# Attention on one core: more exponentials on VectorE, part of its last product on GpSimd, and TensorE's work dealt out in unequal rounds

## The chip, the core and the metric

The kernel runs on one core of a Trainium2 chip. A core has five engines with queues of their own, which run side by side and wait for one another through semaphores: TensorE (PE in the profile, with its weight loads as PEld), VectorE (DVE), ScalarE (ACT), GpSimd (POOL) and SyncE (SP, which here only issues DMAs). The metric is the device time of one execution in microseconds (us); lower is better. Times are quoted as the median of a few runs, and the profile is of one execution.

## The reference, cut to what matters

Multi-query attention: 8 batches, 1024 positions, 16 query heads of 64, and one key and one value head that all query heads share.

```
scores   = q @ k.T / sqrt(64)                     # per batch and head, 1024 x 1024
weights  = exp(scores - max) / sum(exp(scores - max))
attn_out = weights @ v                            # 1024 x 64 per head
```

Everything comes in and goes out as float32. The kernel works in float16 with float32 sums, leaves the maximum out, and checks at the end that no sum has left a safe range; a general version behind a branch would compute the case where one has. The branch is not taken for this data.

## The kernel before, in words

**Steps.** Heads are taken in pairs, queries in chunks of 512, keys in blocks of 128. One *step* is one key block for one chunk of one pair: 64 pairs x 2 chunks x 8 key blocks = 1024 steps (`STEPS`). A batch is 128 steps. In a step TensorE multiplies a key block by the chunk's queries for both heads (two matmuls of 64 rows x 512 columns, L247) and so fills a score tile `sc` of 128 x 1024 float32. `sc` comes from a PSUM pool of three buffers (`scp`), so the scores of step u can only be written when the tile of step u-3 has been read.

**Two ways to the exponential.** Most steps go to ScalarE: one ACTIVATE (L260) reads `sc` and writes `wt`, 128 x 1024 float16. Every fifth step (`VE_EVERY = 5`, `to_vector`) goes to VectorE instead; I call that a *unit*, and there are 200 of them, from step 10 to step 1005. `vector_exp` computes the exponential of a unit from the bits of a float16:

1. the *eviction* (L211): `sc` to 16-bit integers in `w3[:, 1]`, which read as float16 are a piecewise linear exponential;
2. `m` (L217): its mantissa with the exponent set to zero;
3. `w0` (L227): its power of two, into `w3[:, 0]`;
4. the *square* (L235): `m2 = m * m`;
5. the *last product* (L237): `w3[:, 2] = w3[:, 1] * m2`.

The three tiles `w3[:, 0..2]` are weights of the same unit against three scaled copies of the values (`vp[:, 1]`, `vp[:, 0]`, `vp[:, 2]`), so a unit gives TensorE three matmuls where a ScalarE step gives one. The eviction is issued in its step; the other four operations wait in a list, `pend`, and `step` issues two of them per step. The last product of a unit stays in `product` until the next unit and is issued right behind that unit's eviction.

**Values.** `values` multiplies the weights of one head and 128 queries by the value rows: for each *group*, 8 matmuls plus 2 more for each unit among its chunk's 8 steps, all into one column range of a PSUM tile `ot` (L318). There are 1024 groups, as many as steps, and they run 18 steps (`LAG`) behind the scores. Seven groups share an `ot` tile; when it is full, `inverse` (L263, reciprocals of the sums) and `finish` (L272, the division, to `osb`) are put into `pend`. I call the two a *finish*; there are 146.

**The order of the work.** The order on each engine is written out by hand (`manual_schedule`): each engine runs its own instructions in the order of the program text. The main loop goes in rounds of two steps (`BATCH = 2`): both steps' scores, then any new finish, then two groups of values, then `after`, which loads and turns what the next batch needs. Near the end (`HURRY`) values run with less lag. Around the loop stand a start-up (loads, the first transposes) and an end (`last_values`, the check, the flag).

**GpSimd's queue.** It holds, in the program's order, the DMA issues of the queries (`load_q`, L121) and values (`load_v`, L104) of the next batch, and two multiplications (`prep_k`, L190) per batch that make the scaled keys. Nothing else is on it in the main loop. SyncE's queue holds the stores (L300), the key loads and the transposing DMAs.

Of the kernel before, what the change touches and what calls it, by code (L numbers as in the profile page):

```python
# [14 lines left out]
ALU = mybir.AluOpType  # L15
# [6 lines left out]
C0 = 0.9833984375  # L22
C3 = 0.163818359375
CS = 2.1471603163479376
VE_EVERY = 5


@with_exitstack
def attention_main(ctx, tc, q, k, v, out, flag):
# [38 lines left out]
    op = ctx.enter_context(tc.tile_pool(name="op", bufs=2, space=PSUM))  # L68
# [66 lines left out]
    def bank(name):  # L135
        return op.tile([P, 512], FP32, tag="ot", name=name)
# [69 lines left out]
    def vector_exp(sc, p, c, j):  # L206
        w3 = w3p.tile([P, 3, 2, QCH], FP16, tag="w3", name=f"we{p}_{c}_{j}")
        m = mp.tile([P, 2, QCH], FP16, tag="m", name=f"m{p}_{c}_{j}")
        m2 = mp.tile([P, 2, QCH], FP16, tag="m2", name=f"mm{p}_{c}_{j}")
        t = w3[:, 1].bitcast(I16)  # L210
        nc.vector.tensor_scalar(  # L211
            out=t, in0=sc, scalar1=15.0 * 1024, scalar2=0.0, op0=ALU.add, op1=ALU.max
        )
        if product:
            pend.append(product.pop())
        pend.append(
            lambda: nc.vector.tensor_scalar(  # L217
                out=m.bitcast(I16),
                in0=t,
                scalar1=0x3FF,  # L220
                scalar2=0x3C00,
                op0=ALU.bitwise_and,
                op1=ALU.bitwise_or,
            )
        )
        pend.append(
            lambda: nc.vector.tensor_scalar(  # L227
                out=w3[:, 0].bitcast(I16),
                in0=t,
                scalar1=0x7C00,  # L230
                scalar2=None,
                op0=ALU.bitwise_and,
            )
        )
        pend.append(lambda: nc.vector.tensor_tensor(out=m2, in0=m, in1=m, op=ALU.mult))  # L235
        product.append(
            lambda: nc.vector.tensor_tensor(out=w3[:, 2], in0=w3[:, 1], in1=m2, op=ALU.mult)  # L237
        )
        wt[(p, c, j)] = [(w3[:, 0], 1), (w3[:, 1], 0), (w3[:, 2], 2)]

# [21 lines left out]
    def inverse(o, g0, n):  # L262
        nc.vector.reciprocal(out=rec_all[:, g0 : g0 + n], in_=o[:, 0:n, D])  # L263

    def finish(o, g0, n):

        rec = rec_all[:, g0 : g0 + n]
        i0 = g0 % (OCH * GRP)
        if i0 == 0:
            osb[0] = osbp.tile([P, OCH * GRP, D], FP32, tag="osb", name=f"osb{g0}")  # L270
        ob = osb[0]
        nc.vector.tensor_tensor(  # L272
            out=ob[:, i0 : i0 + n, :],
            in0=o[:, 0:n, 0:D],
            in1=rec.unsqueeze(2).broadcast_to([P, n, D]),
            op=ALU.mult,
        )
        while stored[0] < g0 + n:
            e = stored[0]
            e += GRP // 2 if e >= NG - GRP else GRP  # L280
            if e > g0 + n:
                break
            store(ob, stored[0], e)
            stored[0] = e
        per = HP * NCH * GRP
        if g0 + n == NG:
            check(g0 - GRP // 2, NG, ok_all[:, B:])
        elif checked[0] < B and g0 + n >= min((checked[0] + 1) * per, NG - GRP):
            e = min((checked[0] + 1) * per, NG - GRP)
# [16 lines left out]

    def values(p, c, g):

        b = p // HP
        qb, hh = divmod(g, 2)  # L310
        gg = (p * NCH + c) * GRP + g
        if gg % GB == 0:
            ot[0] = bank(f"ot{gg}")[:, 0 : GB * 72].rearrange("p (g f) -> p g f", f=72)
        o = ot[0]
        vp = kv[b]["vp"]
        terms = [(j, w, i) for j in range(NKT) for w, i in wt[(p, c, j)]]
        for n, (j, w, i) in enumerate(terms):
            nc.tensor.matmul(  # L318
                o[:, gg % GB, 0 : D + 1],
                w[:, hh, qb * P : (qb + 1) * P],  # L320
                vp[:, i, j, 0 : D + 1],
                start=(n == 0),
                stop=(n == len(terms) - 1),
            )
        if gg % GB == GB - 1 or gg == NG - GRP - 1:
            late.append((o, gg - gg % GB, gg % GB + 1))
        if g == GRP - 1:
            for j in range(NKT):
                del wt[(p, c, j)]

    def last_values():

# [39 lines left out]
    LAG = 2 * NKT + 2  # L372
    STEPS = NP * NCH * NKT
    PSTEPS = NCH * NKT
    BATCH = 2
    LAST_VE = (STEPS - 2 * NKT) // VE_EVERY * VE_EVERY
    HURRY = STEPS - NKT - 4

    def to_vector(u):
        return u % VE_EVERY == 0 and NKT <= u <= LAST_VE  # L380

    def step(u):
        p, r = divmod(u, PSTEPS)
        c, j = divmod(r, NKT)
        scores(p, c, j, to_vector(u))
        for _ in range(2):
            if pend:
                pend.pop(0)()
        if product and u >= LAST_VE + 2 and not pend:
            product.pop()()  # L390

    def after(u):
        p, r = divmod(u, PSTEPS)
# [24 lines left out]
    with tc.manual_schedule():  # L418
        load_kv(0)
        load_q_first(0)  # L420
        make_identity(nc, ident)
        for p in range(1, NFIRST):
            load_q_first(p)
        load_v(0)
        for c in range(NKT):
            load_q(0, c)
        for t in vps:
            for i, ci in enumerate((1.0, C0, C3)):
                nc.gpsimd.memset(t[:, i, :, D : D + 1], ci)
# [12 lines left out]
        first_k_out(kps, 1)  # L442
        nc.vector.tensor_copy(out=q0[:, NKT // 2 :, :], in_=qf[:, NKT // 2 :, :])
        prep_v(0)
        for c in range(NKT):
            turn_q(0, c)
        nxt = 0
        for u0 in range(0, STEPS, BATCH):
            us = range(u0, u0 + BATCH)
            for u in us:  # L450
                step(u)
            for f in late:
                pend.insert(0, lambda f=f: inverse(*f))
                pend.insert(min(2, len(pend)), lambda f=f: finish(*f))
            del late[:]
            for _ in range(2 * BATCH):
                if u0 < HURRY:
                    ready = nxt < u0 + BATCH - LAG
                else:
                    ready = nxt < STEPS - GRP and nxt // GRP * NKT + NKT + 4 <= u0  # L460
                if ready:
                    pa, ra = divmod(nxt, PSTEPS)
                    values(pa, *divmod(ra, NKT))
                    nxt += 1
            for u in us:
                after(u)
# [135 lines left out]
```

## Time and profile before

| what | value |
|---|---|
| time, median of 3 runs | 782.43 us (781.96 to 783.74) |
| the profiled execution, its own time | 783.46 us |
| its span, first to last instruction | 781.5 us |
| mean granted TensorE clock | 0.990 |
| first ScalarE exponential starts, last one ends | 7.35 us, 774.00 us |
| first eviction starts, last one starts | 15.49 us, 756.73 us |

The profile page gives for each engine its busy time and its share of the span, then groups of equal instructions with their summed busy time, the mean length of one and the idle time ahead of them. Successive instructions of one engine overlap a little (the next one starts before the last one's end is recorded), so the price of an instruction in a full queue is the distance from its start to the next start, which the timeline shows, and not its recorded length. The chain of waits tells who waited for whom.

### The profile page before, as it was taken

The page shows a single profiled execution, that of the slowest core. Times are in us where ns is not written, and L with a number is a line of the kernel's source. Part 1 is how long each engine was busy: PE and PEld are TensorE (multiplying, and loading weights), DVE is VectorE, ACT ScalarE, POOL GpSimd, SP SyncE. Part 2 cuts the span into 40 slices and gives each one's busy share as a digit, 9 for nine tenths or more (in the row PEclk, how much of TensorE's full clock was granted, in tenths as well). Part 3 has the DMA queues.
Part 4 walks back from the last instruction along what each step waited for, and adds up shares of the span by engine and source line. Part 5 has one row for each costly group of instructions (what it writes and reads, how often), then busy time and mean ns, then how long its engine had stood idle before and what let it go on. Part 6 is the DMA issues. An engine that isn't in the chain of part 4 may idle for free.

```text
span 781.5 us, 30669 instructions
## 1 busy us (share of the span) xinstructions
PE 728.7 (93%) x13474; PEld 474.1 (61%) x13474; DVE 728.9 (93%) x1349; ACT 762.5 (98%) x827; POOL 65.9 (8%) x99
## 2 busy tenths in 40 slices
PE   5999999999999999999999999999999999999996
PEld 2566666656666666666656666666666666666665
DVE  3899999999999999999999999999999999999992
ACT  7999999999999999999999999999999999999996
POOL 4210002100011002010020100201002100000000
PEclk8899999999999999999999999999999999999999
DMA  9949118582193813756155552556417373111113
GB/s 169 146 93 164 55 44 157 97 136 57 29 170 76 154 33 76 150 103 115 45 91 123 124 95 56 90 128 115 101 42 125 89 149 71 51 35 55 43 43 84
DMA packets 168633, 73.84 MB, mean 94 GB/s; under 512 B 93744, under 2 KB 161328, under 8 KB 168496
## 3 DMA queue, kind: packets, MB, share of 16 engines
q1 hardware_dynamic: 148864, 53.76, 32.5%
q0 software_dynamic: 18576, 17.57, 14.8%
q8 instruction: 106, 1.74, 1.0%
q10 hardware_dynamic: 1056, 0.52, 0.3%
q14 instruction: 31, 0.25, 0.1%
HBM read 37.75 MB, written 33.55 MB: 91 GB/s over the span
## 4 chain that ended last, share of the span: by engine, by line
ACT 38%; DVE 21%; PE 21%; issue 19%; DMA 1%; DVEq 0%; ACTq 0%
ACT wt L260 38%; PE ot L318 11%; PE sc L247 9%; DVE we L211 8%; DVE osb L272 3%; DVE we L237 3%; DVE mm L235 3%; DVE m L217 2%; DVE we L227 2%; DVE rec_all L263 1%; DMA qf<-in_q_dram 1%; PE otl L344 0%; DVE both L366 0%; DVE ok_all L370 0%; DVE ge L360 0%
## 5 line engine op out<-in xcount | busy, mean ns | idle before, releaser
L260 ACT ACTIVATE wt<-sc 128x1024 f16<-128x1024 f32 x824 | 760.0, 1062 | 7.4 <-PE sc L247 6.1
L318 PE MATMUL ot<-vp,wt 128*128 128x65 f16 x6528 | 418.4, 194 | 0.6 <-issue 0.6
L318 PEld LDWEIGHTS <-wt 128*128 128x128 f16 x6528 | 325.8, 98 | 114.8 <-issue 114.8
L247 PE MATMUL sc<-qt,k2t 64*128 64x512 f16 x2048 | 352.8, 386 | 41.2 <-ACT wt L260 29.1
L318 PE MATMUL ot<-vp,we 128*128 128x65 f16 x4800 | 352.2, 193 | 0.0
L318 PEld LDWEIGHTS <-we 128*128 128x128 f16 x4800 | 250.0, 97 | 30.6 <-issue 30.6
L211 DVE TENSOR_SCALAR we<-sc 128x1024 int16<-128x1024 f32 x200 | 243.6, 1218 | 23.2 <-PE sc L247 22.1
L247 PEld LDWEIGHTS <-k2t 64*128 64x128 f16 x2048 | 93.2, 94 | 149.0 <-issue 111.0
L237 DVE TENSOR_TENSOR we<-we,mm 128x1024 f16<-128x1024 f16 x200 | 136.9, 685 | 0.0
L235 DVE TENSOR_TENSOR mm<-m 128x1024 f16<-128x1024 f16 x200 | 136.5, 683 | 0.0
L272 DVE TENSOR_TENSOR osb<-ot,rec_all 128x448 f32<-128x448 f32 x146 | 90.5, 620 | 4.2 <-DVE rec_all L263 0.2
L217 DVE TENSOR_SCALAR m<-we 128x1024 int16<-128x1024 int16 x200 | 85.8, 429 | 0.0
L227 DVE TENSOR_SCALAR we<-we 128x1024 int16<-128x1024 int16 x200 | 83.5, 418 | 0.0
L104 POOL DMA_DIRECT2D vp<-in_v_dram x8 | 7.5, 936 | 388.5 <-PE ot L318 388.4
L121 POOL DMA_DIRECT2D q<-in_q_dram x64 | 35.0, 571 | 26.7 <-DMA qt<-q 22.9
L263 DVE RECIPROCAL rec_all<-ot 128x7 f32<-128x7 f32 x146 | 28.6, 196 | 8.7 <-PE ot L318 8.6
L190 POOL TENSOR_SCALAR k16d<-knat 128x512 f16<-128x512 f32 x14 | 21.4, 1537 | 134.7 <-DMA knat<-in_k_dram 134.7
L202 DVE TENSOR_SCALAR vp<-vp 128x512 f16<-128x512 f16 x16 | 3.9, 286 | 2.0 <-DMA vp<-in_v_dram 2.0
L155 PE MATMUL kps<-ident,k 128*64 128x128 f16 x16 | 1.3, 314 | 4.5 <-DVE k L146 4.5
L184 DVE COPY qt<-qps 128x512 f16<-128x512 f16 (+1 forms) x2 | 1.1, 554 | 3.3 <-PE qps L171 3.3
L155 PEld LDWEIGHTS <-k 128*64 128x64 f16 x16 | 0.8, 159 | 4.7 <-DVE k L146 4.7
L436 ACT ACT_TABLE_LOAD x1 | 1.3, 1283 | 1.9 <-issue 1.9
(29 smaller groups left out, 22.2 us busy)
## 6 DMA issues: line engine op xcount, KB each, us to landing
out_dram<-osb SPq DMA_DIRECT2D x127, 256.0 KB, 2.4
q<-in_q_dram POOLq DMA_DIRECT2D x56, 256.0 KB, 8.8
knat<-in_k_dram SPq DMA_DIRECT2D x7, 256.0 KB, 4.1
q<-in_q_dram POOLq DMA_DIRECT2D x8, 192.0 KB, 8.0
vp<-in_v_dram POOLq DMA_DIRECT2D x8, 128.0 KB, 4.4
qt<-q SPq DMA_TRANSPOSE x64, 3.9
qf<-in_q_dram ACTq DMA_DIRECT2D x2, 256.0 KB, 4.4
knat<-in_k_dram SPq DMA_DIRECT2D x2, 128.0 KB, 3.8
```

Of the source, the lines that this page charges most:

```text
L121: nc.gpsimd.dma_start(out=q16[(b, c)], in_=q[b, c * P : (c + 1) * P, h0:, :].rearrange("p h d -> p (h d)"),)
L190: nc.gpsimd.tensor_scalar(out=k16d[:, :, i, :], in0=st["knat"], scalar1=kscale, scalar2=None, op0=ALU.mult)
L211: nc.vector.tensor_scalar(out=t, in0=sc, scalar1=15.0 * 1024, scalar2=0.0, op0=ALU.add, op1=ALU.max)
L217: lambda: nc.vector.tensor_scalar(out=m.bitcast(I16), in0=t, scalar1=0x3FF, scalar2=0x3C00, op0=ALU.bitwise_and, op1=ALU.bitwise_or,)
L227: lambda: nc.vector.tensor_scalar(out=w3[:, 0].bitcast(I16), in0=t, scalar1=0x7C00, scalar2=None, op0=ALU.bitwise_and,)
L235: pend.append(lambda: nc.vector.tensor_tensor(out=m2, in0=m, in1=m, op=ALU.mult))
L237: lambda: nc.vector.tensor_tensor(out=w3[:, 2], in0=w3[:, 1], in1=m2, op=ALU.mult)
L247: nc.tensor.matmul(sc[:, hh, :], k2t[r : r + 64, j * P : (j + 1) * P], qt[b][r : r + 64, p % HP, c * QCH : (c + 1) * QCH], start=True, sto ...
L260: nc.scalar.activation(out=w, in_=sc, func=EXP, scale=escale, bias=math.log(CS))
L263: nc.vector.reciprocal(out=rec_all[:, g0 : g0 + n], in_=o[:, 0:n, D])
L272: nc.vector.tensor_tensor(out=ob[:, i0 : i0 + n, :], in0=o[:, 0:n, 0:D], in1=rec.unsqueeze(2).broadcast_to([P, n, D]), op=ALU.mult,)
L318: nc.tensor.matmul(o[:, gg % GB, 0 : D + 1], w[:, hh, qb * P : (qb + 1) * P], vp[:, i, j, 0 : D + 1], start=(n == 0), stop=(n == len(terms ...
```

## The change: what it does

- **Units.** Steps with `u * 2 % 9 < 2`, that is `u % 9` of 0 or 5, are units: two in every nine steps, 223 in all, from step 9 to step 1008, at distances of 5 and 4 steps in turn. ScalarE is left with 801 steps.
- **The last product is split by columns.** Of its 1024 columns VectorE computes the first 384 (`VE_U`) where it computed all before. The other 640 go to GpSimd, issued directly behind the square.
- **TensorE's rounds.** A round no longer has two steps throughout. In a period of nine steps the rounds end after steps 1, 2, 5, 6 and 8 (`DEAL`), so they hold 2, 1, 3, 1 and 2 steps. `plan` fixes how many value matmuls have been issued by each round's end, so that each of the five rounds carries the same share of values, counted in matmuls; a round may end in the middle of a group. `values` therefore returns a list of single matmuls.
- A new finish is put into `pend` at a round's end with at most one other operation between its two halves; the last steps (`HURRY`) begin two steps earlier and their condition for values is written for single steps.

```diff
-VE_EVERY = 5
+DEAL = (0, 1, 1, 0, 0, 1, 1, 0, 1)
+DEAL_AT = 0
+VE_U = 384
+VE_N = 2
+VE_M = 9
...
-        pend.append(lambda: nc.vector.tensor_tensor(out=m2, in0=m, in1=m, op=ALU.mult))
+        we, wu, mm = (x.rearrange("p h q -> p (h q)") for x in (w3[:, 1], w3[:, 2], m2))
+
+        def square():
+            nc.vector.tensor_tensor(out=m2, in0=m, in1=m, op=ALU.mult)
+            nc.gpsimd.tensor_tensor(
+                out=wu[:, VE_U:], in0=we[:, VE_U:], in1=mm[:, VE_U:], op=ALU.mult
+            )
+
+        pend.append(square)
         product.append(
-            lambda: nc.vector.tensor_tensor(out=w3[:, 2], in0=w3[:, 1], in1=m2, op=ALU.mult)
+            lambda: nc.vector.tensor_tensor(
+                out=wu[:, :VE_U], in0=we[:, :VE_U], in1=mm[:, :VE_U], op=ALU.mult
+            )
         )
...
-    BATCH = 2
-    LAST_VE = (STEPS - 2 * NKT) // VE_EVERY * VE_EVERY
-    HURRY = STEPS - NKT - 4
+    LAST_VE = max(u for u in range(STEPS - 2 * NKT + 1) if u * VE_N % VE_M < VE_N)
+    HURRY = STEPS - NKT - 6
     def to_vector(u):
-        return u % VE_EVERY == 0 and NKT <= u <= LAST_VE
+        return NKT <= u <= LAST_VE and u * VE_N % VE_M < VE_N
...
+    def plan():
+        upto = [0]
+        for g in range(STEPS):
+            many = sum(to_vector(g // GRP * NKT + j) for j in range(NKT))
+            upto.append(upto[-1] + NKT + 2 * many)
+        due = {}
+        for u in range(STEPS):
+            if u >= HURRY:
+                if u % 2:
+                    due[u] = None
+                continue
+            n, i = divmod(u - DEAL_AT, len(DEAL))
+            if DEAL[i]:
+                at = DEAL_AT + len(DEAL) * (n + sum(DEAL[: i + 1]) / sum(DEAL)) - LAG
+                at = max(at, 0.0)
+                g = int(at)
+                due[u] = round(upto[g] + (at - g) * (upto[g + 1] - upto[g]))
+        return due
...
-        for u0 in range(0, STEPS, BATCH):
-            us = range(u0, u0 + BATCH)
-            for u in us:
-                step(u)
+        for u in range(STEPS):
+            step(u)
+            us.append(u)
+            if u not in due:
+                continue
+            new = []
             for f in late:
-                pend.insert(0, lambda f=f: inverse(*f))
-                pend.insert(min(2, len(pend)), lambda f=f: finish(*f))
+                new += [lambda f=f: inverse(*f), lambda f=f: finish(*f)]
+            if len(new) == 2:
+                new[1:1] = pend[:1]
+                del pend[:1]
+            pend[:0] = new
             del late[:]
...
+            if due[u] is not None:
+                while made < due[u]:
+                    if not todo:
+                        todo = values(nxt)
+                        nxt += 1
+                    todo.pop(0)()
+                    made += 1
```

More of the change, by code (lines that the diff above doesn't have):

```diff
@@ L305, in store, with values @@
         )
-    def values(p, c, g):
-        b = p // HP
+    def values(gg):
+        p, c = divmod(gg // GRP, NCH)
+        g = gg % GRP
         qb, hh = divmod(g, 2)
-        gg = (p * NCH + c) * GRP + g
         if gg % GB == 0:
@@ L314, in values, with one @@
         o = ot[0]
-        vp = kv[b]["vp"]
+        vp = kv[p // HP]["vp"]
         terms = [(j, w, i) for j in range(NKT) for w, i in wt[(p, c, j)]]
-        for n, (j, w, i) in enumerate(terms):
+        def one(n, j, w, i):
+            last = n == len(terms) - 1
             nc.tensor.matmul(
@@ L322, in values @@
                 start=(n == 0),
-                stop=(n == len(terms) - 1),
+                stop=last,
             )
[L325 to L329, printed above, removed]
+            if not last:
+                return
+            if gg % GB == GB - 1 or gg == NG - GRP - 1:
+                late.append((o, gg - gg % GB, gg % GB + 1))
+            if g == GRP - 1:
+                for x in range(NKT):
+                    del wt[(p, c, x)]
+        return [lambda n=n, t=t: one(n, *t) for n, t in enumerate(terms)]
     def last_values():
@@ L446, in attention_main @@
             turn_q(0, c)
-        nxt = 0
-        for u0 in range(0, STEPS, BATCH):
-            us = range(u0, u0 + BATCH)
-            for u in us:
-                step(u)
-            for f in late:
-                pend.insert(0, lambda f=f: inverse(*f))
-                pend.insert(min(2, len(pend)), lambda f=f: finish(*f))
-            del late[:]
[L456 to L466, printed above, removed]
+        nxt = made = 0
+        todo = []
+        due = plan()
+        us = []
+        for u in range(STEPS):
[4 more added lines that the diff above has]
+            new = []
+            for f in late:
+                new += [lambda f=f: inverse(*f), lambda f=f: finish(*f)]
[3 more added lines that the diff above has]
+            pend[:0] = new
+            del late[:]
+            if due[u] is not None:
[5 more added lines that the diff above has]
+                    made += 1
+            else:
+                for _ in range(4):
+                    if not todo and nxt < STEPS - GRP and nxt // GRP * NKT + NKT + 3 <= u:
+                        todo = values(nxt)
+                        nxt += 1
+                    for f in todo:
+                        f()
+                    todo = []
+            for x in us:
+                after(x)
+            us = []
         assert nxt == STEPS - GRP
```

## The prediction, made before the change was run

> **What bounds the kernel now.** I read the page's busy shares first, then the groups, then the waits.
>
> ```profile
> PE 728.7 (93%) x13474; PEld 474.1 (61%) x13474; DVE 728.9 (93%) x1349; ACT 762.5 (98%) x827; POOL 65.9 (8%) x99
> ...
> L260 ACT ACTIVATE wt<-sc 128x1024 f16<-128x1024 f32 x824 | 760.0, 1062 | 7.4 <-PE sc L247 6.1
> L211 DVE TENSOR_SCALAR we<-sc 128x1024 int16<-128x1024 f32 x200 | 243.6, 1218 | 23.2 <-PE sc L247 22.1
> L190 POOL TENSOR_SCALAR k16d<-knat 128x512 f16<-128x512 f32 x14 | 21.4, 1537 | 134.7 <-DMA knat<-in_k_dram 134.7
> ```
>
> ScalarE hardly ever waits (7.4 us), so the time is close to its 824 exponentials. VectorE and TensorE are not far behind: VectorE waits 23.2 us ahead of its evictions. The waits by pairs:
>
> ```profile
> PE sc L247 <- ACT wt L260: 29.1, 96, 0.5
> DVE we L211 <- PE sc L247: 22.1, 45, 1.3
> PE sc L247 <- DVE we L211: 7.6, 19, 0.9
> ```
>
> TensorE waits for a free score buffer, mostly ScalarE's. That is a chain led by ScalarE with VectorE close behind. The prices per instruction are start-to-start distances in the timelines. ScalarE, then a VectorE unit:
>
> ```profile
> 177.91 29.44 ACT L260 ACTIVATE wt<-sc 128x1024 f16<-128x1024 f32 x32 [0.36 <-PE sc L247]
> ```
> ```profile
> 303.18 1.21 DVE L211 TENSOR_SCALAR we<-sc 128x1024 int16<-128x1024 f32 x1
> 304.31 0.68 DVE L237 TENSOR_TENSOR we<-we,mm 128x1024 f16<-128x1024 f16 x1
> 304.91 0.42 DVE L217 TENSOR_SCALAR m<-we 128x1024 int16<-128x1024 int16 x1
> 305.24 0.42 DVE L227 TENSOR_SCALAR we<-we 128x1024 int16<-128x1024 int16 x1
> 305.58 0.68 DVE L235 TENSOR_TENSOR mm<-m 128x1024 f16<-128x1024 f16 x1
> 306.18 0.20 DVE L263 RECIPROCAL rec_all<-ot 128x7 f32<-128x7 f32 x1
> 306.41 0.62 DVE L272 TENSOR_TENSOR osb<-ot,rec_all 128x448 f32<-128x448 f32 x1
> 306.95 1.21 DVE L211 TENSOR_SCALAR we<-sc 128x1024 int16<-128x1024 f32 x1
> ```
>
> One exponential: (29.44 - 1.06) / 31 = 0.9155 us. VectorE: eviction 1.13, last product 0.60, m 0.34, w0 0.34, square 0.60, so 3.01 a unit; a finish 0.23 + 0.54 = 0.77 (0.65 where its halves lie apart, a fifth of them; 0.74 on the mean). TensorE: in the timeline one pair of score matmuls to the first value matmul is 0.33 us (318.74 to 319.07), two pairs 0.53 (319.80 to 320.33), so three about 0.74. A round's 24 value matmuls take 0.84 and 20 take 0.74, so n take 0.24 + 0.025 n.
>
> **The budget of the stretch from the first to the last eviction** (15.49 to 756.73, 741.2 us, 995 steps), per ten steps:
> - ScalarE 8 x 0.9155 = 7.32.
> - VectorE 2 x 3.01 + 10/7 x 0.74 = 7.08, and 0.15 for scaling values, the checks and its delays behind GpSimd (about 15 us in the stretch): 7.23.
> - TensorE five rounds of 0.53 + 0.80 (22.4 matmuls): 6.65.
>
> Measured: 741.2 / 99.5 = 7.45, that is 0.13 above the largest. So the three are coupled through three score buffers, at a loss of some 13 us.
>
> **The change part by part.**
>
> *Units.* ScalarE loses 23 exponentials: 23 x 0.9155 = 21.1 us. Per nine steps it now has 7 x 0.9155 = 6.41.
>
> *The last product.* The 1024-column one is recorded with 0.685 us. A float16 copy by VectorE (L184) is recorded with 0.417 for 512 columns and 0.691 for 1024, the same pace, so a column costs 0.54 ns and an instruction 0.14. That makes 0.35 recorded for 384 columns, and 0.27 in a full queue, where 0.08 overlap as they do now (0.685 against 0.60). The unit falls from 3.01 to 2.68. VectorE per nine steps: 2 x 2.68 + 9/7 x 0.74 + 0.13 = 6.44. Over the stretch that is 6.44 x 111 = 715 us, where it was 7.23 x 99.5 = 719: 23 more units take back what the shorter product gives.
>
> *TensorE.* Two more matmuls for eight groups and 23 units: 368, so 20.7 a round, 0.76 us. Rounds of 1, 2 and 3 steps: 2 x 0.33 + 2 x 0.53 + 0.74 + 5 x 0.76 = 6.26. In the round of three (u % 9 = 3, 4, 5) the unit's scores come last and wait until ScalarE has freed the buffer of step 2; that round's values, and the next scores, are queued behind.
>
> *The product on GpSimd.* No two-input arithmetic on GpSimd is in the trace. From below: the 128-column select on it in the start-up takes 0.29 us against 0.10 for a memset of one column, 1.5 ns a column, so 1.05 us for 640. From above: L190 takes 1.478 us for 512 columns of one input, 2.9 ns a column: 1.85 us, and 3.7 if a second input doubles it. I take 1.85, as L190 is the nearest row. The Trainium skill (GPSIMD Engine Reference, Performance versus the Vector engine) measures a tensor_tensor of 2048 float32 at 4497 ns; an estimate from that page for 640 columns is 1.4 us, which no run here shows and which would leave the sum as it is. GpSimd is then busy 223 x 1.85 + 66 = 479 us of some 770, so it is no bound.
>
> *What GpSimd's queue holds behind the product*, which waits for the square: the query and value loads and L190. So far the queue runs ahead: the value load of a batch fires as soon as TensorE has left the buffer (213.37, 308.10). Now it comes in its place in the program, 30 steps or 22 us later, and VectorE scales those values only 40 steps after that; the query loads come 16 steps (11.7 us) before SyncE turns them, and land in 8.8. If they come late, the turning and the stores behind it on SyncE's queue wait; the turned queries are needed 50 steps (37 us) after their turning, which covers it. TensorE first reads a unit's third tile 11 steps or more (8 us) after its scores; the chain is about 3.5 on VectorE and 2 on GpSimd. Behind the two L190 it would be 3 us more, a stall of a microsecond at seven places at worst. Price of all this: zero to 7 us, taken as 0.
>
> *VectorE against GpSimd.* Here the two have met 14 times:
>
> ```profile
> 145.20 2.94 POOL L190 TENSOR_SCALAR k16d<-knat 128x512 f16<-128x512 f32 x2 [22.38 <-DMA knat<-in_k_dram]
> ```
> ```profile
> 145.23 0.86 DVE L227 TENSOR_SCALAR we<-we 128x1024 int16<-128x1024 int16 x1
> 146.01 0.68 DVE L235 TENSOR_TENSOR mm<-m 128x1024 f16<-128x1024 f16 x1
> 146.61 0.19 DVE L263 RECIPROCAL rec_all<-ot 128x7 f32<-128x7 f32 x1
> 146.84 0.62 DVE L272 TENSOR_TENSOR osb<-ot,rec_all 128x448 f32<-128x448 f32 x1
> 147.38 1.22 DVE L211 TENSOR_SCALAR we<-sc 128x1024 int16<-128x1024 f32 x1
> ```
>
> w0 at the start of the first L190 takes 0.86 instead of 0.42, held about 0.44 us; the square inside the same L190 takes its usual 0.68; finish and eviction, which read PSUM, run at their usual length. So GpSimd keeps VectorE out while it reads (0.44 us for 512 columns), not for its whole length. At 242.37 and 334.87 m takes 0.69 instead of 0.42, 1.07 us after an L190 began, so there is a second, shorter hold when it writes. The new product starts about 0.1 us after the square; 640 columns of two inputs held at the same rate are 1.1 us. In VectorE's order, of 222 squares 110 are followed by a finish and the eviction in either order (1.90 us) before the next last product, and 112 by the eviction alone (1.13 us, plus any idle time). So the reads are just covered. Bounds: nothing; or, if VectorE is kept out to the product's end, 0.1 + 1.85 - 1.13 = 0.82 us at 112 units, 92 us. I take 0, nearer to the row in which the square ran through an L190 undelayed.
>
> *The coupling.* ScalarE 6.41, VectorE 6.44, TensorE 6.26: three engines within 3%, where they were 7.32, 7.23 and 6.65, within 10%. VectorE's four-step units with a finish need 3.33 to 3.45 us against 2.75 of ScalarE's, so it swings by 0.7 us. The loss grows; bounds are 0.13 (as now) and 0.26 (doubled). I take 0.18: 6.62 per nine steps, x 111 = 735 us against 741.2.
>
> **Sum.** 741.2 to 735 gives -6.2; the first unit comes one step earlier (-0.9) and 15 instead of 18 ScalarE steps follow the last (-2.7): -9.8. From the profiled execution's 783.46 this is 773.7; the median of the runs lies 1.0 below the profiled execution, so 772.5.
>
> **The rivals.**
> - *VectorE is held by GpSimd and becomes the bound (slower).* Place: the last product, m and w0 behind an eviction with no finish near, 112 units. For it: the second hold at 242.37, which 640 columns would lengthen to 0.35 us, and m and w0 come 1.4 to 2.1 us after the square, when a 1.85 us product writes. Against it: idle time ahead of the eviction covers it where there is any. It turns the sign from about 0.2 us at each of these (22 us on 715, with a coupling loss of 8, is the 744.8 that makes no change). At 0.4 us: 715 + 45 + 8 = 768, so 783.5 + 26.8 - 3.6 - 1.0 = 805.7.
> - *Held for the whole product.* With 0.82 us at the 112 units and 0.1 + 1.85 - 1.90 = 0.05 at the other 110: 715 + 92 + 6 + 5 (coupling) = 818, so 783.5 + 76.8 - 4.6 = 855.7 us; a product over 3.3 us on GpSimd itself would end there too (223 x 3.7 = 825). The square inside L190 speaks against it. This is the rule of the Trainium skill (SBUF — State Buffer, Who interferes with whom): the shared port pair is locked exclusively for the whole instruction, against two-port and two-input VectorE instructions. By that rule the time is 856; the trace agrees only for the first 0.44 us of an L190.
> - *Nothing gained.* The coupling loss doubles to 0.27 per nine steps: 6.71 x 111 = 745, 782 us. For it: VectorE has no slack left over ScalarE. Against: the present loss arises with a slack of only 0.1 in ten steps.
>
> **How the numbers follow.** Less than 0.2% (1.6 us) can't be told from no change. Forecast (762 to 780): 0.53. Held at part of the units (784 to 830): 0.29. Held for the whole product: 0.09. Nothing gained: 0.09, of which 0.06 within 0.2%, 0.01 below and 0.02 above. So faster 0.54, same 0.06, slower 0.40. The range begins at 762, where the loss is 0.09 per nine steps (6.53 x 111 = 725; at the present 0.13 it would be 767), and reaches to 812, which takes in a hold of 0.45 us at the 112 units; some 0.15 lie above and 0.03 below.
>
> **What would show it.** ScalarE busy some 21 us less and idle more; last product near 0.35 us recorded; m and w0 at 0.42 and last product undelayed would show the ports free; m, w0 or last product longer by tenths, and ScalarE waiting for scores that wait for the eviction, would show the first rival. GpSimd's product length decides between 1.05 and 3.7. The prediction is wrong if holds exceed 0.2 us a unit, or if TensorE's short rounds leave evictions waiting.

## The result, and the profile after

The change makes the kernel slower: 807.08 us, median of 5 runs (806.21 to 808.46), against 782.88 (781.96 to 783.98) for the kernel before beside it. The ratio is 1.0309, with a 95% interval of 1.0291 to 1.0326. The forecast was 772.5; the first rival, VectorE held by GpSimd, had 805.7. One run of the experiment split_only (806.39 us) was in a slow state and is left out of what is said below.

The page of the kernel after: busy shares, the chain by engine and by line, and the groups (busy time, mean ns of one, idle time ahead and its cause).

```profile
PE 749.3 (93%) x13842; PEld 496.7 (62%) x13842; DVE 768.5 (95%) x1464; ACT 755.9 (94%) x804; POOL 380.2 (47%) x322
...
DVE 70%; PE 19%; issue 6%; ACT 4%; DMA 1%; DVEq 0%; ACTq 0%
...
L274 ACT ACTIVATE wt<-sc 128x1024 f16<-128x1024 f32 x801 | 753.5, 1043 | 39.7 <-PE sc L261 34.7
L243 POOL TENSOR_TENSOR we<-we,mm 128x640 f16<-128x640 f16 x223 | 311.6, 1397 | 407.2 <-DVE mm L242 173.7
...
L215 DVE TENSOR_SCALAR we<-sc 128x1024 int16<-128x1024 f32 x223 | 271.1, 1216 | 9.9 <-PE sc L261 8.4
...
L249 DVE TENSOR_TENSOR we<-we,mm 128x384 f16<-128x384 f16 x223 | 113.7, 510 | 0.0
```

The waits by pairs (total us, times, longest):

```profile
PE sc L261 <- DVE we L215: 35.0, 52, 2.4
ACT wt L274 <- PE sc L261: 34.7, 61, 2.2
...
DVE we L215 <- PE sc L261: 8.4, 11, 2.1
...
PE sc L261 <- ACT wt L274: 3.3, 14, 0.3
```

The lead has passed from ScalarE to VectorE. TensorE waited 29.1 us for ScalarE's score buffers and 7.6 for VectorE's; now it is 3.3 and 35.0. ScalarE idles 39.7 us where it idled 7.4, and VectorE waits only 9.9 us ahead of its evictions. The last product of 384 columns (L249) has a mean of 510 ns, though 350 was expected. The mean hides two lengths. VectorE's timeline, one unit without a finish between the square and the next last product, then one with a finish:

```profile
301.88 0.68 DVE L242 TENSOR_TENSOR mm<-m 128x1024 f16<-128x1024 f16 x1
302.48 1.22 DVE L215 TENSOR_SCALAR we<-sc 128x1024 int16<-128x1024 f32 x1
303.62 0.70 DVE L249 TENSOR_TENSOR we<-we,mm 128x384 f16<-128x384 f16 x1
304.24 0.41 DVE L221 TENSOR_SCALAR m<-we 128x1024 int16<-128x1024 int16 x1
...
305.51 0.19 DVE L277 RECIPROCAL rec_all<-ot 128x7 f32<-128x7 f32 x1
305.74 0.62 DVE L286 TENSOR_TENSOR osb<-ot,rec_all 128x448 f32<-128x448 f32 x1
306.28 1.21 DVE L215 TENSOR_SCALAR we<-sc 128x1024 int16<-128x1024 f32 x1
307.41 0.35 DVE L249 TENSOR_TENSOR we<-we,mm 128x384 f16<-128x384 f16 x1
```

GpSimd's timeline at the same time:

```profile
302.71 1.40 POOL L243 TENSOR_TENSOR we<-we,mm 128x640 f16<-128x640 f16 x1 [2.12 <-DVE mm L242]
305.73 1.40 POOL L243 TENSOR_TENSOR we<-we,mm 128x640 f16<-128x640 f16 x1 [1.63 <-PE sc L261]
```

GpSimd begins 0.23 us after the eviction (302.71 against 302.48). VectorE's last product follows 1.14 us after the eviction, at 303.62, and takes 0.70 instead of 0.35: it is kept out until 303.97, that is 1.26 us into the 1.40 of GpSimd's instruction. With a finish in between it comes at 307.41, when GpSimd is done, and takes 0.35. Of the 223 last products 114 are recorded with 0.35 us, 86 with about 0.7, and the rest mostly between; forecast were 112 units with nothing but the eviction in between, and 110 with a finish.

**The account of the stretch from the first to the last eviction.** It lasts from 15.51 to 785.00 us, 769.5 where it was 741.2. VectorE's work as the prediction had it is 715. The holds of the last product are 223 x (0.510 - 0.350) = 36 us. The scaling of the values (L206, a mean of 637 ns where it was 286, 16 times) and the first instruction of the checks (626 where it was 215, 7 times) lose another 8.5; these, too, are held by GpSimd:

```profile
77.15 1.47 DVE L206 TENSOR_SCALAR vp<-vp 128x512 f16<-128x512 f16 x1
```
```profile
77.06 1.42 POOL L243 TENSOR_TENSOR we<-we,mm 128x640 f16<-128x640 f16 x1
```

Unheld, this instruction takes 0.28 us, so it was let in at 78.34, 1.28 us into GpSimd's. Ahead of evictions VectorE waits 9.9 us. That adds up to 769. The end behind the last eviction is 3.2 us shorter: 783.46 + 28.3 - 3.2 = 808.6, and the profiled execution took 808.46.

### The profile page after: what moved, and what is told of

Read it like the earlier page. It is cut to its first block, busy times and chain, and to the rows that moved or that the text cites. A ratio compares the mean times of both kernels' runs of the same rounds, so it can differ in the third digit from the quotient of the medians.

```text
span 806.6 us, 32093 instructions
## 1 busy us (share of the span) xinstructions
PE 749.3 (93%) x13842; PEld 496.7 (62%) x13842; DVE 768.5 (95%) x1464; ACT 755.9 (94%) x804; POOL 380.2 (47%) x322
## 4 chain that ended last, share of the span: by engine, by line
DVE 70%; PE 19%; issue 6%; ACT 4%; DMA 1%; DVEq 0%; ACTq 0%
DVE we L215 26%; DVE mm L242 13%; PE ot L335 11%; DVE osb L286 9%; DVE we L249 9%; PE sc L261 8%; DVE m L221 7%; ACT wt L274 3%; DVE we L231 2%; DVE rec_all L277 2%; DVE vp L206 1%; DMA qf<-in_q_dram 1%; DVE ge L381 0%; DMA out_dram<-osb 0%; DVE both L387 0%
## 5 line engine op out<-in xcount | busy, mean ns | idle before, releaser
L274 ACT ACTIVATE wt<-sc 128x1024 f16<-128x1024 f32 x801 | 753.5, 1043 | 39.7 <-PE sc L261 34.7
L243 POOL TENSOR_TENSOR we<-we,mm 128x640 f16<-128x640 f16 x223 | 311.6, 1397 | 407.2 <-DVE mm L242 173.7
L335 PE MATMUL ot<-vp,wt 128*128 128x65 f16 x6344 | 431.8, 195 | 2.9 <-issue 2.4
L335 PE MATMUL ot<-vp,we 128*128 128x65 f16 x5352 | 393.5, 194 | 0.6 <-issue 0.5
L335 PEld LDWEIGHTS <-we 128*128 128x128 f16 x5352 | 289.4, 97 | 59.8 <-issue 59.5
L215 DVE TENSOR_SCALAR we<-sc 128x1024 int16<-128x1024 f32 x223 | 271.1, 1216 | 9.9 <-PE sc L261 8.4
L242 DVE TENSOR_TENSOR mm<-m 128x1024 f16<-128x1024 f16 x223 | 153.8, 690 | 0.0
L249 DVE TENSOR_TENSOR we<-we,mm 128x384 f16<-128x384 f16 x223 | 113.7, 510 | 0.0
L231 DVE TENSOR_SCALAR we<-we 128x1024 int16<-128x1024 int16 x223 | 94.4, 423 | 0.0
L221 DVE TENSOR_SCALAR m<-we 128x1024 int16<-128x1024 int16 x223 | 94.1, 422 | 0.0
L206 DVE TENSOR_SCALAR vp<-vp 128x512 f16<-128x512 f16 x16 | 9.6, 637 | 0.9 <-DMA vp<-in_v_dram 0.9
```

What stands on the lines that cost most here:

```text
L215: nc.vector.tensor_scalar(out=t, in0=sc, scalar1=15.0 * 1024, scalar2=0.0, op0=ALU.add, op1=ALU.max)
L221: lambda: nc.vector.tensor_scalar(out=m.bitcast(I16), in0=t, scalar1=0x3FF, scalar2=0x3C00, op0=ALU.bitwise_and, op1=ALU.bitwise_or,)
L231: lambda: nc.vector.tensor_scalar(out=w3[:, 0].bitcast(I16), in0=t, scalar1=0x7C00, scalar2=None, op0=ALU.bitwise_and,)
L243: nc.gpsimd.tensor_tensor(out=wu[:, VE_U:], in0=we[:, VE_U:], in1=mm[:, VE_U:], op=ALU.mult)
L249: lambda: nc.vector.tensor_tensor(out=wu[:, :VE_U], in0=we[:, :VE_U], in1=mm[:, :VE_U], op=ALU.mult)
L274: nc.scalar.activation(out=w, in_=sc, func=EXP, scale=escale, bias=math.log(CS))
```

## The experiments

Each time is the median of its runs, with the ratio to the kernel before run beside it (782 to 783 us) and its interval. "Holds" are what VectorE's timeline shows over the length of an instruction that is not held, and "the stretch" is the time from the first to the last eviction.

**What GpSimd's reading holds.** First the second input is taken away.

```diff
-            nc.gpsimd.tensor_tensor(
-                out=wu[:, VE_U:], in0=we[:, VE_U:], in1=mm[:, VE_U:], op=ALU.mult
-            )
+            nc.gpsimd.tensor_scalar(
+                out=wu[:, VE_U:], in0=mm[:, VE_U:], scalar1=2.0, scalar2=None, op0=ALU.mult
+            )
```

> The GpSimd product is replaced by a multiplication of the same 640 columns of the square by a constant: one input read in place of two, so the third weights of the 223 units are not those of the reference. Theory (GpSimd's reading keeps VectorE's last product out): one input is read in about half the 1.26 us, which the eviction covers, so the last product is recorded with 0.35 us in nearly all units (now 0.35 in 114 of 223 and about 0.70 in most of the rest, mean 0.51), the stretch of evictions falls from 769.5 us by about 36, and the time to about 772. Rival 1 (VectorE is kept out to the end of the GpSimd instruction): one-input multiplications were longer per column in the kernel before (1.48 us for 512), so the instruction grows to about 1.85 us, the last product to 1.0 us or more at half the units, and the time to 830 or more. Rival 2 (the three engines are coupled too tightly, the hold only fills idle time): last product shorter, but the time stays above 800.

Measured: 820.74 us, 1.0486 (1.0444 to 1.0528). The last product is freed as the theory said, 217 of 223 at 0.35 us, but the time went the other way. VectorE and GpSimd in one unit:

```profile
306.05 1.22 DVE L215 TENSOR_SCALAR we<-sc 128x1024 int16<-128x1024 f32 x1
307.18 0.35 DVE L249 TENSOR_TENSOR we<-we,mm 128x384 f16<-128x384 f16 x1
307.45 0.93 DVE L221 TENSOR_SCALAR m<-we 128x1024 int16<-128x1024 int16 x1
```
```profile
306.29 1.81 POOL L243 TENSOR_SCALAR we<-mm 128x640 f16<-128x640 f16 x1 [1.66 <-DVE mm L242]
```

The instruction is longer (1.81 us), the last product runs undelayed inside it, and now m is held, for 0.51 us, until 307.96: 1.67 us after GpSimd began. That is the second hold, which the kernel before showed at 242.37 and which I took for GpSimd's write. The starts in VectorE's timeline put about 60 us of holds on m and w0 in the stretch. So with one input nothing is locked out for GpSimd's whole length, and my expectation left the second hold out. With two inputs m is not held (304.24, 0.41), but it also starts after GpSimd's instruction has ended (302.71 + 1.40 = 304.11), so that says nothing of a second hold there.

**What the offload is worth.** All 1024 columns on VectorE, the rest as in the change.

```diff
-VE_U = 384
+VE_U = 1024
...
-            nc.gpsimd.tensor_tensor(
-                out=wu[:, VE_U:], in0=we[:, VE_U:], in1=mm[:, VE_U:], op=ALU.mult
-            )
```

> Two units in nine and the unequal rounds stay, VectorE computes all 1024 columns of the last product. Theory: VectorE is the bound, so the time follows its work: last product 0.60 instead of 0.27 in a full queue (222 x 0.33 = 74 us more), holds of the last product (36 us) and of the small instructions (about 10 us) gone: stretch about 797 us, time about 835. Rival 2 (coupling): VectorE's work isn't what sets the time, so it stays within 10 us of 807.

Measured: 824.98 us, 1.0522 (1.0489 to 1.0556). The stretch is 787.9 us, and VectorE waits 2.8 us ahead of evictions in all of it: its instructions alone make the time. The theory's 835 missed by 10. I had added the 74 us to a stretch in which VectorE waited 9.9 us ahead of its evictions; that it now waits 2.8 makes 7 of the 10, and what made the rest stays open. The prices of the prediction fit better (715 + 74 = 789). Of the 74 us that the offload takes from VectorE, 18 arrive in the time.

**The size of GpSimd's part**, in the kernel after and (with earlier loads, below) at two more sizes.

```diff
-VE_U = 384
+VE_U = 576   # cols448, cols448_early; 512 in cols512_early, 192 in cols832_early
```

> The kernel after with 448 instead of 640 columns on GpSimd, 576 on VectorE. Theory A: GpSimd's reading, 1.26 us for 640 columns, is about 0.88 us and begins 0.23 us after the eviction's start, so it ends inside the eviction (1.13 us) and the last product is never held; it costs 0.10 us more at 222 units (22 us) and saves 36: 791 to 798. Rival (the whole instruction and its write keep VectorE out, or VectorE's total doesn't decide): 805 or more.

Measured: 786.33 us, 1.0063 (1.0040 to 1.0087). The holds of the last product are gone, as expected (0.37 us from its start to the next at the median, 0.65 at most), and the time is 5 us better than the range.

> As cols448_early (779 us, no holds), 512 columns on GpSimd. If GpSimd's reading keeps the last product out, 1.97 ns a column from 0.23 us after the eviction's start, it ends at 1.24 us: the last product is held 0.11 us at the 110 or so units without a finish next to the eviction (12 us), VectorE saves 0.033 us at 222 (7 us): 782 to 786. Without such a slope (a hold that is there or not): 805 or 772.

Measured: 788.23 us, 1.0073 (1.0056 to 1.0089), 2 us above the range; the holds of the last product are the 12 us expected.

> As cols448_early, 832 columns on GpSimd. Reading ends at 1.87 us: the last product held 0.74 us at some 110 units (81 us), the units with a finish next to the eviction (1.90 us) still free; VectorE saves 0.20 us at 222 (44 us): stretch about 777, time 812 to 822. Without the slope: below 805.

Measured: 826.83 us, 1.0564 (1.0547 to 1.0582), 5 us above the range; holds of the last product 78 us, 81 expected. Held last products and GpSimd's instructions beside them, 512 columns:

```profile
300.90 1.22 DVE L215 TENSOR_SCALAR we<-sc 128x1024 int16<-128x1024 f32 x1
302.04 0.53 DVE L249 TENSOR_TENSOR we<-we,mm 128x512 f16<-128x512 f16 x1
```
```profile
301.13 1.15 POOL L243 TENSOR_TENSOR we<-we,mm 128x512 f16<-128x512 f16 x1 [2.36 <-DVE mm L242]
```

and 832 columns:

```profile
309.21 1.22 DVE L215 TENSOR_SCALAR we<-sc 128x1024 int16<-128x1024 f32 x1
310.34 0.96 DVE L249 TENSOR_TENSOR we<-we,mm 128x192 f16<-128x192 f16 x1
```
```profile
309.44 1.76 POOL L243 TENSOR_TENSOR we<-we,mm 128x832 f16<-128x832 f16 x1 [1.71 <-DVE mm L242]
```

Unheld, 512 and 192 columns take 0.42 and 0.25 us on VectorE. So VectorE is let in 1.02, 1.26 and 1.61 us after GpSimd began on 512, 640 and 832 columns: 1.84 ns a column and a little fixed time. For 448 that is 0.90, and with the start at 0.23 it ends just inside the eviction. The hold grows with the columns as a reading would. But at each size it also ends 0.13 to 0.15 us before the recorded end of GpSimd's instruction, and the scaling of values above was let in 0.14 us before it. So with two inputs these runs can't tell a hold by the reading from one that lasts for all but the end of the instruction; only with one input the two come apart.

**The last product ahead of the eviction.**

```diff
         def square():
             ...
+            nc.vector.tensor_tensor(
+                out=wu[:, :VE_U], in0=we[:, :VE_U], in1=mm[:, :VE_U], op=ALU.mult
+            )
         pend.append(square)
-        product.append(
-            ...
-        )
```

> The kernel after with VectorE's 384 columns of the last product issued right behind the square, ahead of the next eviction. Theory A: VectorE's part now takes the port first (0.27 us), GpSimd reads behind it, until about 0.35 + 1.26 us after the square, while the next instruction that needs the port is m at 0.27 + 1.13: m held about 0.2 us at the 112 units without a finish in between, 22 us instead of 36: 788 to 798. Rival: the wait of the last product for the square just issued costs as much as it saves: 803 or more.

Measured: 818.12 us, 1.0441 (1.0421 to 1.0461). The rival holds. No last product is held (222 of 223 at 0.36 us), GpSimd's becomes 1.50 us instead, but two instructions now read what the one ahead of them has just written:

```profile
305.51 0.68 DVE L242 TENSOR_TENSOR mm<-m 128x1024 f16<-128x1024 f16 x1
306.23 0.36 DVE L247 TENSOR_TENSOR we<-we,mm 128x384 f16<-128x384 f16 x1
...
307.27 1.21 DVE L215 TENSOR_SCALAR we<-sc 128x1024 int16<-128x1024 f32 x1
308.52 0.43 DVE L221 TENSOR_SCALAR m<-we 128x1024 int16<-128x1024 int16 x1
```

Square to last product is 0.72 us where a square takes 0.60, and eviction to m 1.25 where an eviction takes 1.13. This is no hold: GpSimd's product, from 306.33 on, was over before m. The two times 0.12 us at some 200 units are about 48 us, more than the 36 saved. VectorE also waits 13.3 us ahead of evictions, 3.4 more than in the kernel after, 9.7 of them in two of TensorE's stalls that the next experiments are about. Together that comes to 15 us, and the stretch grew by 14.5, to 784.0.

**TensorE's rounds, and GpSimd's queue.** Even rounds in the kernel after, then earlier loads.

```diff
-DEAL = (0, 1, 1, 0, 0, 1, 1, 0, 1)
+DEAL = (0, 1)
```

> The kernel after with rounds of two steps throughout. Theory: TensorE has room, the rounds are not what costs: within 4 us of 807. Rival 2 (rounds of one and three make evictions or exponentials wait): 800 or less.

Measured: 818.23 us, 1.0431 (1.0388 to 1.0474): neither theory. TensorE's waits for which the profile names no cause (`issue`, ahead of scores and values) are 16.6 us, with one of 5.3; in the kernel after they are 4.3, before the change 0.6.

The split alone, in the kernel before:

```diff
+VE_U = 384
...
-        pend.append(lambda: nc.vector.tensor_tensor(out=m2, in0=m, in1=m, op=ALU.mult))
-        product.append(
-            lambda: nc.vector.tensor_tensor(out=w3[:, 2], in0=w3[:, 1], in1=m2, op=ALU.mult)
-        )
+        # square() and the two parts of the product as in the change
```

> The kernel before (200 units, rounds of two) with only the last product split, 384 columns on VectorE and 640 on GpSimd. Theory: VectorE saves 66 us and loses about 30 to holds (0.35 us at the 87 units without a finish next to the eviction), so it has slack, ScalarE stays the bound with 824 exponentials of 0.9155 us, and part of its 12 us of waits goes: 774 to 781. Rival: holds push single evictions late enough to stop ScalarE whatever VectorE's total, 786 or more.

Measured: 795.63 us, the median of three runs (793.99 to 798.98); the interval of the ratio is 1.0145 to 1.0283. The theory missed, and the rival's 786 or more holds. VectorE has slack (busy 685 us of 792), and what its waits show is, besides the holds, a stall of TensorE:

```profile
DVE we L212 <- PE sc L258: 76.1, 91, 6.3
...
ACT wt L271 <- PE sc L258: 18.2, 21, 5.9
...
PE sc L258 <- issue: 5.7, 1, 5.7
```

It ends at 73.19 us. The DMA view from 60 to 75 us, in 40 slices (busy tenths of the engines, and GB/s):

```profile
DMA  9999900000009997999999699779994456999997
GB/s 310 311 256 82 30 14 12 14 15 14 14 12 36 220 76 29 62 62 47 60 87 108 84 109 100 82 111 200 126 141 76 72 114 47 33 177 293 214 34 171
...
qt<-q SPq DMA_TRANSPOSE x3, 10.9
```

Transposes land 10.9 us after their issue (3.9 at the median of the kernel before), at a time when the DMA engines are busy and yet move 12 to 15 GB/s.

What TensorE waited for shows in the records of another DMA queue, the one that loads instructions in pieces of 16 KB. The pages of the kernels before and after have it so:

```profile
q8 instruction: 106, 1.74, 1.0%
```
```profile
q8 instruction: 109, 1.79, 0.9%
```

TensorE has 26948 instructions before and 27684 after, 254 for each piece in both, so the pieces are most likely its own. They land some 7 us apart, at most 10.5 in the kernel before. In split_only none lands between 58.11 and 71.87 us, and TensorE goes on at 73.19, 1.32 us after that. In the traces of all 20 kernels TensorE has 26 waits of over 0.5 us without a named cause, and 23 of them end 1.26 to 1.63 us after such a piece has landed. A count settles it: in 25 of the 26, with n pieces landed before the late one, TensorE stood after 444 + 255.7 n instructions, to within about 1, wherever in the run that was; and nowhere did it get further than that ahead of a piece. So TensorE had run out of loaded instructions. That the piece was late because the loads and transposes filled the DMA engines fits the view above, and what follows, but no run changes the instruction loads by themselves.

Before the change GpSimd ran ahead and had issued the next batch's loads long before the transposes; now they wait in the queue behind each unit's product. So I moved the loads 24 steps up:

```diff
-            at = hp * PSTEPS + r - 3 * PSTEPS
+            at = hp * PSTEPS + r - 24
             ...  # load_kv, load_v, load_q
-            at -= PSTEPS
+            at -= 4 * PSTEPS - 24
```

> The kernel after with the query and value loads of the next batch issued 24 steps earlier in the program (from step 24 of a batch instead of 48), so that they no longer stand in GpSimd's queue right before the transposing DMAs and overlap with them. Theory A (VectorE, held by GpSimd's reads of the last product's port, is the bound): the holds stay at 35 us, VectorE has only some 16 us of idle time in 769, of which a part goes: 800 to 806. Theory B (the late loads, through the DMA engines and TensorE's stalls, are the larger cost): 790 or less.

Measured: 805.04 us, 1.0287 (1.0270 to 1.0304). Theory A: in the kernel after the loads cost some 2 us, a difference within the two intervals.

> The kernel before with the product split 384 and 640, and the same earlier loads. Theory B (what made split_only slower than the kernel before, with VectorE only 685 us busy, is TensorE's stalls of up to 5.7 us while loads and transposes share the DMA engines): TensorE's waits for nothing that the profile shows fall from 11.6 us to under 3, and the time to 774 to 781. Rival (the product on GpSimd itself delays the chain): 788 or more, with the stalls gone or not.

Measured: 785.73 us, 1.0040 (1.0025 to 1.0054), and the runs lie within 1 us. Some 10 of the 13 us that the split had added are gone, and so are the stalls (no wait without a named cause is left); the range was still missed by 5 us.

> As split_early (one unit in five, rounds of two), with 448 columns on GpSimd. Open: why relieving VectorE alone did not help (786). If the holds did it, which push single evictions late: 781 or less, as the holds are gone. If ScalarE is the bound with 824 exponentials and its waits come from TensorE's rounds: 783 to 787.

Measured: 778.12 us, 0.9944 (0.9927 to 0.9960). So what split_early had kept was the holds: without them the split and the earlier loads are worth 4 us even at the old share of units. No run moves the loads alone in the kernel before; its waits without a named cause are only 0.6 us, so they can't be worth much there.

> Rounds of two steps throughout and the earlier loads, all else as in the kernel after. Open from rounds_two (818 us): whether the even rounds or TensorE's stalls of up to 5.7 us while loads and transposes share the DMA engines cost the 11 us. Stalls: with the earlier loads they are gone, and it comes within 4 us of the 805 of after_early. Rounds: 812 or more.

Measured: 805.64 us, 1.0276 (1.0203 to 1.0348). As the stall theory said: with 640 columns even rounds cost nothing that can be seen (the stretch is 765.8 us here and 765.7 in after_early), and the 818 of rounds_two was the loads.

> 448 columns on GpSimd and the earlier loads. Theory (VectorE's total is the bound; the loads cost some 2 us in the kernel after): 781 to 786. Rival (TensorE's stalls are the rest of the loss): 778 or less.

Measured: 778.82 us, 0.9934 (0.9908 to 0.9961), 2 us below the range and just above the rival's. The loads cost 7.5 us here, against cols448, not 2. Its chain and its evictions:

```profile
DVE 84%; issue 6%; PE 5%; ACT 2%; DMA 2%; DVEq 0%
...
L215 DVE TENSOR_SCALAR we<-sc 128x1024 int16<-128x1024 f32 x223 | 271.1, 1216 | 2.5 <-PE sc L261 2.5
L249 DVE TENSOR_TENSOR we<-we,mm 128x576 f16<-128x576 f16 x223 | 100.4, 450 | 0.0
```

With no hold, VectorE works through its stretch of 740.2 us with 2.5 us of waits, and the kernel of the change, with 192 columns moved back and the loads moved up, is faster than the kernel before.

**What rounds cost without holds.** The same kernel with `DEAL = (0, 1)`:

> 448 columns, earlier loads, two units in nine, but rounds of two steps throughout. Theory C (TensorE's rounds cost nothing as long as VectorE alone is the bound, which it is in cols448_early, where no eviction waits): 776 to 783. Rival (the unequal rounds are what lets the units run without waits): 785 or more.

Measured: 792.06 us, 1.0123 (1.0107 to 1.0140). The rival holds and theory C falls: the unequal rounds are worth 13 us here. The evictions wait 11.7 us where they waited 2.5, TensorE waits 17.6 us for ScalarE's buffers where it waited 5.4.

Then fewer units, first with even rounds and then with rounds that stand to the units as the change's do. I call these rounds *locked* to the units:

```diff
-VE_N = 2
-VE_M = 9
+VE_N = 3     # u3of14; u4of19 has 4 and 19
+VE_M = 14
-DEAL = (0, 1, 1, 0, 0, 1, 1, 0, 1)
+DEAL = (0, 1)
+DEAL = (0, 1, 1, 0, 0, 1, 1, 1, 0, 0, 1, 1, 0, 1)                    # u3of14_locked
+DEAL = (0, 1, 1, 0, 0, 1, 1, 1, 0, 0, 1, 1, 1, 0, 0, 1, 1, 0, 1)     # u4of19_locked
```

> Three units in fourteen steps (215), 448 columns on GpSimd, earlier loads, rounds of two. Per VectorE's total: 214 x 2.78 + 104 for finishes + about 25 for the rest = 724 us, where cols448 has 8 units and 22 us more at a stretch of 745; ScalarE 999 x 11/14 x 0.9155 = 719. If VectorE's total was the bound: a stretch of 730 to 738 and a time of 772 to 780. If the loss lies in the coupling of the engines: 782 or more.

Measured: 780.74 us, 0.9954 (0.9925 to 0.9983), between the two ranges. Its evictions wait 21.8 us.

> Four units in nineteen steps (211), else as u3of14. VectorE 210 x 2.78 + 129 = 713 us, ScalarE 998 x 15/19 x 0.9155 = 721: ScalarE is the larger now, a stretch of 731 to 740, a time of 773 to 781. Coupling: 782 or more.

Measured: 789.31 us, 1.0074 (1.0047 to 1.0101): fewer units than u3of14, and slower, by the coupling. Its evictions wait 38.4 us.

> As u3of14 (215 units), with rounds in a period of fourteen steps that stand to the units as those of the change do: 2, 1, 3, 1, 1, 3, 1, 2 steps. Theory C: here no engine alone is the bound, so the rounds decide whether evictions wait (21.8 us in u3of14): 768 to 777. Rival (the loss is in the close budgets, not in the rounds): 778 to 784.

Measured: 773.34 us, 0.9881 (0.9865 to 0.9898), the fastest of all, and theory C. Its waits:

```profile
DVE we L215 <- PE sc L261: 12.6, 24, 1.5
PE sc L261 <- ACT wt L274: 9.7, 48, 0.3
...
ACT wt L274 <- PE sc L261: 1.9, 5, 0.7
```

> As u4of19 (211 units), with rounds of 2, 1, 3, 1, 1, 3, 1, 1, 3, 1, 2 steps. Theory C: 770 to 782. Rival: 785 or more, as u4of19 (789).

Measured: 776.57 us, 0.9918 (0.9901 to 0.9935), theory C again. With the rounds locked to the units 211 units gain 13 us and 215 gain 7. ScalarE waits 1.9 us for scores in u3of14_locked: it is the bound again, and VectorE nearly so. The unequal rounds are also shorter, 1.7 to 1.8 steps on the mean instead of 2. No run shifts them against the units, so how much of the gain is the phase and how much the shorter rounds stays open.

## Why the prediction was wrong

- **VectorE against GpSimd: the step that failed.** It read "So the reads are just covered" and took a price of 0. By its own figures they were not quite covered: 0.1 + 1.1 is 0.07 us more than the eviction's 1.13, some 8 us at 112 units. The mechanism, the place (the last product at the 112 units with nothing but the eviction behind the square) and the even balance that makes it count were in the text. The size of the term was wrong: GpSimd starts 0.23 us after the eviction instead of the estimated 0.1, and keeps VectorE out for 1.26 us instead of 1.1, so 0.35 us stick out. That is 36 us, with 8.5 more at the small instructions, against about 22 that it took to turn the sign. The first rival named this and came to 805.7 against 807.08. It was wrong in m and w0, which are not held here, and that it came so close is partly luck: it had 45 us of holds and 8 of coupling where 36, 8.5 and 9.9 us of waits were measured.
- **The whole instruction.** By the rule of the Trainium skill (SBUF — State Buffer, Who interferes with whom) VectorE is locked out until the instruction ends. For this product the trace nearly agrees, 1.26 of 1.40 us, and as nearly at the other sizes; for the one-input instruction it doesn't, as a last product ran undelayed inside it. My price for that rival (856) came from a product of 1.85 us, the step below. The argument against it, a square that ran through L190, came from a one-input instruction and did not carry over to a product of two.
- **The product on GpSimd.** 1.85 us was taken, from the one-input L190; it is 1.40. The nearest row by kind was the wrong one: on 640 columns a one-input multiplication takes 1.81 us, longer than a two-input product. The estimate from the Trainium skill (GPSIMD Engine Reference, Performance versus the Vector engine), 1.4, is what was measured.
- **VectorE's own prices** were right: 0.27 us for 384 columns, 2.68 for a unit (the shortest units of the kernel after are 2.67), 715 us for the stretch without holds. From cols448_early, 740 - 222 x 0.10 gives 718, with 2.5 of waits in it.
- **The coupling** was charged with 20 us. Where VectorE is the bound and the rounds are the change's, it is next to nothing (2.5 us of waits in cols448_early); with even rounds it is 13. The run closest to the balance that was forecast is u3of14_locked, with 724 us of work on VectorE and 719 on ScalarE; its stretch is 734.4, so it loses about 10. So the 20 was too much as far as the runs show; what two units in nine would lose with the reads covered, no run shows.
- **GpSimd's queue** was taken as 0 between 0 and 7; it is some 2 us here, and was 7.5 in cols448, 10 in split_only and 12 in rounds_two. The prediction asked only whether these loads land in time. What cost the time, loads and transposes on the DMA engines at once and TensorE's instructions that come late, was not in it.
- **The first unit** did not come earlier (15.51 us against 15.49), and ScalarE's recorded busy time fell by 6.5 us, not 21, because exponentials that stand apart are recorded without overlap.

## What to carry to other kernels

Before work is moved to an engine that shares a port with the engine it relieves, lay the time for which it holds the port against the work that doesn't need the port and stands right behind it; cut the piece so that it ends inside (448 columns here, not 640), as each column past that point costs more than it saves (1.84 ns at half of the units against 0.54 ns at all). An idle queue that runs ahead does a service that ends when it gets work in the middle of the loop: move its early DMA issues up in the program. When two or three engines are within a few per cent of each other, how the rounds are laid to the units is worth as much as the balance (7 to 13 us here).

## What the hardware showed that I had not expected

- GpSimd holds VectorE's port in a pattern that depends on the instruction. Two inputs: one hold, 1.02, 1.26 and 1.61 us for 512, 640 and 832 columns of float16, which ends 0.13 to 0.15 us before the instruction does. One input: the last product ran freely 0.9 us after the start, and m was held up to 1.67 us of 1.81. That the second hold is the write is inferred.
- On 640 columns GpSimd takes 1.81 us for a multiplication by a constant and 1.40 for a product of two tiles.
- A VectorE instruction that reads what the one ahead of it wrote starts 0.12 us later than one that doesn't (1.25 against 1.13, 0.72 against 0.60).
- TensorE stood for up to 5.7 us with no cause named by the profile, and went on 1.3 us after a late 16 KB load of instructions had landed; by count it had used up what was loaded. That moving the query and value loads up ends such waits is shown by split_early and rounds_two_early, which have none.
